# Moving a block inverse, small copies and squares between GpSimd, VectorE and ScalarE, and a planner that tracks reuse, in a hybrid RWKV-7 and retention decoder layer

## The chip, the core and the metric

The kernel runs on one core of a Trainium2 chip. A core has TensorE (matrix products into PSUM banks), VectorE (DVE), ScalarE (ACT), GpSimd (POOL) and SyncE (SP, which issues all DMAs here); each works through its own instructions in the order in which they are written, and they wait for each other on semaphores. The metric is the device time of one execution in microseconds; the kernel before takes 1558.78 us (median of three runs, the fastest 1557.02).

## What is computed

One layer of a decoder for 304 token rows: 16 meta tokens, a prompt of 256 and 8 samples of 4 tokens.

```python
xn = rms_norm(x, norm_mix)
z = xn @ w_in                       # 2048 -> 3360 + 4096 columns
o_a, S_a = rwkv7_mixer(z_a, ...)    # 16 heads of 64, delta rule state
o_b, S_b = retention_mixer(z_b, ...)  # 4 heads of 256
h = x + concat([o_a, o_b]) @ w_out
hn = rms_norm(h, norm_ffn)
h = h + (silu(hn @ w_gate) * (hn @ w_up)) @ w_down   # 5632 wide
y = rms_norm(h, norm_final)
```

The RWKV part is, per head and token, `S = S * w + (S a) b^T + v k^T` and `out = S r`. The kernel does it in blocks ("units") of 64 tokens (the first of 16), which needs the inverse of a unit lower triangular 64 x 64 matrix for each unit and head.

## The kernel before, in words

All activations are held transposed: features on the 128 partitions, the 304 (later 288) tokens in the free dimension. `main` (L634) walks over all weights in one fixed sequence (`steps`, L123): input projections in the order of `ORDER` (L54: the RWKV head pairs p0 to p7, the retention heads r0 to r3 and their gates g0 to g3 mixed), then the output projection, then the feed-forward part. A weight tile of 128 x 128 is used in three matmuls, because every fp32 value is split into a rounded half and a rest: hi x xh, hi x xl, lo x xh. ScalarE makes the half (`cast`, L617: the tile `wh`, four batches of 512 columns ahead, five buffers) and VectorE the rest (`rest`, L629: the tile `wl`). Weights come by SP into three buffers of 1024 columns (`wr`). Results collect in two PSUM banks, `acc`; the six other banks, `mm`, are for everything else. Nearly all other tiles lie in one arena, which the profile calls `arena_dt.float` (`arena_dt.float32r` for the rounded halves), so it can't tell them apart by name. All instructions are recorded by one helper, so they have one line, L302.

Beside `main` run streams, written as Python generators; each `yield` is a place where another stream, or `main`, may be written next. A pair of RWKV heads is the stream `pair` (L906): decays, normalised keys, clearing and filling the operand tiles (the fills are ScalarE copies, L988 to 993, and GpSimd copies, L995 to 1004), score matrices, then `inverse` (L1095), `units` (L1172, five units one after the other, a chain of small matmuls and copies), `sample` (L1219, the 8 decode sequences) and `pair_out` (L1297, group norm and gate). `mixed` (L803) shifts and mixes the projected rows of the RWKV part, and copies the last rows to `shout`, an output. `ret` (L1379) is a retention head. These streams all run beside the input projections, in the first 600 us; the output projection begins shortly before that.

`inverse` works on 5 units of a pair at a time, both heads on the partitions, 128 x [5, 64]. It cuts the diagonal 16 x 16 blocks out (`rb`, L1101, one `tensor_reduce`, L1106), forms their inverse by 15 steps of substitution, and combines blocks to 32 and to 64 by matmuls (L1150 to 1169). In the substitution, VectorE spreads row s of the blocks over the partitions by `stream_shuffle` (15 of 80 columns, in three groups of five), and GpSimd does, for each s, a multiply and an add on 5 x (15 - s) columns, which each need the one before.

`rsqrt` (L705) gives 1/sqrt by an integer estimate and two steps of Newton's kind, all on VectorE, nine instructions. It is called once for the first norm (304 columns), in each pair for the keys (312 columns, with `floor`) and for the group norm (288), in each retention head (288), and twice on three columns (`rstd_from`, L1556).

The order is set by `Plan` (L307). The kernel is built twice. In the draft, `book` (L348) gives every instruction a start and an end, from a cost for each engine, from when the engine is free, and from when what its operands hold is ready; `pick` (L426) writes the next step of the first stream that is due by TensorE's clock, and otherwise a step of `main`. The second time the same choices are replayed and the arena's places are those that `Room` found from the draft's times. Two things in it matter here. `follows` (L334) is meant to make a new use of a PSUM bank or a buffer wait for the last use of what lay there, and `banks` to know which tiles lie in PSUM. Both are keyed by tile names: `t` (L573) hands in the name that it asks for (`mm_0`), while `book` looks up the name that the tile carries, to which the allocator has appended a running number (`mm_0_58`). So neither is ever found, and the planner takes reused banks and buffers as free at once.

Of the kernel before, what the change touches and what calls it, by code (L numbers as in the profile page):

```python
# [12 lines left out]
ALU = mybir.AluOpType  # L13
# [293 lines left out]
class Plan:  # L307
# [5 lines left out]
    def __init__(self, nc, rooms, draft, log, keep):  # L313
# [5 lines left out]
        self.mode, self.parts, self.empty, self.begun, self.idle = None, {}, 0.0, 0.0, 0.0  # L319
        self.streams, self.made = [], 0  # L320
# [27 lines left out]
    def book(self, eng, what, a, k):  # L348
# [20 lines left out]
        else:  # L369
            part = out.shape[0] < P  # L370
            each = sum(math.prod(x.shape[1:]) == 1 for x in ins) if n > 1 else 0
            if eng == "DVE":
                big = max(math.prod(x.shape[1:]) for x in aps)
                per = 0.56 if what == "tensor_scalar" and ins[0].name not in self.banks else 1.05
                dur, tail = {"stream_shuffle": (148, 90), "transpose": (95 + 1.02 * n, 80), "tensor_reduce": (40 + 1.8 * big, 85),
                             "tensor_tensor_scan": (65 + 2.1 * n, 85)}.get(what, (62 + per * n + 67 * each, 83))
            elif eng == "ACT":
                dur, tail = 108 + 0.83 * n + 90 * each - 40 * (ins[0].name in self.banks), 94
            else:
                dur, tail = (60 + 0.85 * n, 60) if what == "memset" else (185 + 0.8 * n, 60) if what == "tensor_copy" else (265 + 2 * n, 60)  # L380
# [14 lines left out]
        self.end = max(self.end, done + 100)  # L395

# [142 lines left out]
class Step:  # L539
# [33 lines left out]
    def t(self, shape, tag, dt=F32, bufs=None, pool=None):  # L573
        self.n += 1
        if pool is not None:
            name = f"{tag}_{self.n}"
            if tag in ("mm", "acc"):
                self.plan.banks.add(name)
            old = self.tags.setdefault(tag, [])
            old.append(name)  # L580
            n = {"mm": 8 - ACC, "acc": ACC}.get(tag, bufs)
            if n and len(old) > n:
                self.plan.follows(name, old[-1 - n])
            return pool.tile(shape, dt, tag=tag, name=name, **({} if bufs is None else {"bufs": bufs}))
# [120 lines left out]
    def rsqrt(self, src, scale, eps, floor=None, out=None):  # L705


        dve = self.dve
# [24 lines left out]
    def start(self):  # L733
# [3 lines left out]
        self.dve.memset(self.ones, 1.0)  # L737
        xh, xl = self.xh, self.xl
# [1031 lines left out]
```

## Time and profile before

| | us |
|---|---|
| median of the runs | 1558.78 |
| the profiled execution's own time | 1558.99 |
| its span, first to last instruction | 1557.1 |
| TensorE busy, in the span | 1535.6 |
| VectorE busy | 1102.0 |
| ScalarE busy | 821.4 |
| GpSimd busy | 179.2 |

The profile's page names engines as PE (TensorE's matmuls), PEld (its weight loads, which overlap them), DVE, ACT, POOL and SP. A row of a group reads: line, engine, operation, written tile <- read tiles, shape and count, then busy us, mean ns of one, and idle us of that engine just before, with who ended it. Matmuls are pipelined and their ends are modelled, so a busy PE can still stand for parts of a microsecond. A row of the waits reads: who waited <- for whom: us in total, times, longest. fp32 matmuls of the `mm` kind are recorded as two passes.

### The profile page before, as it was taken

What the parts mean: (1) busy time and instruction counts of PE and PEld (TensorE: products, weight loads), DVE (VectorE), ACT (ScalarE), POOL (GpSimd) and SP (SyncE); (2) the same over time, 40 slices, a digit from 0 to 9 for tenths busy, and PEclk for the clock granted to TensorE, in tenths of its full rate; (3) what the DMA queues carried; (4) which work ended last, traced back from release to release, by engine and by line L of the source; (5) the groups of instructions that cost most, each with busy time, mean ns of one, the idle gap of its engine ahead of it and who ended that gap; (6) DMA issues with size and microseconds to landing.
All of it is one profiled execution on the core that took longest, in us unless ns stands there. A gap on an engine that the chain in (4) does not pass through costs nothing.

```text
span 1557.1 us, 30803 instructions
## 1 busy us (share of the span) xinstructions
PE 1535.6 (99%) x11388; PEld 1505.7 (97%) x11388; DVE 1102.0 (71%) x2590; ACT 821.4 (53%) x1795; POOL 179.2 (12%) x567
## 2 busy tenths in 40 slices
PE   9999999999999999999999999999999999999997
PEld 8999999998999999999999999999999999999997
DVE  7999888996999786676555565555565656565657
ACT  6766776766676555455444444444444444444445
POOL 0454415513143000000000000000000000000000
PEclk9999999999999999999999999999999999999999
DMA  7443443434545546755555555555555555555553
GB/s 249 154 136 119 127 130 120 115 107 152 181 143 176 170 143 238 243 167 161 164 173 163 174 156 172 162 165 169 168 163 172 164 166 164 171 166 166 161 176 118
DMA packets 76997, 252.48 MB, mean 162 GB/s; under 512 B 9392, under 2 KB 14640, under 8 KB 76848
## 3 DMA queue, kind: packets, MB, share of 16 engines
q1 hardware_dynamic: 76848, 250.52, 51.5%
q8 instruction: 90, 1.47, 0.4%
q14 instruction: 59, 0.48, 0.1%
HBM read 236.21 MB, written 14.28 MB: 161 GB/s over the span
## 4 chain that ended last, share of the span: by engine, by line
PE 85%; DVE 11%; issue 1%; ACT 1%; DMA 1%; POOL 0%; SPq 0%; DVEq 0%; ACTq 0%; POOLq 0%
PE acc L302 76%; PE mm L302 9%; DVE arena_dt.float L302 8%; DVE wl L302 3%; ACT arena_dt.float L302 1%; DMA arena_dt.float<-xT 0%; POOL arena_dt.float L302 0%; DMA arena_dt.float<-lora 0%; ACT wh L302 0%; DVE arena_dt.float32r L302 0%; DMA wr<-big 0%; ACT arena_dt.float32r L302 0%; SPq L302 0%; DVEq L1766 0%; ACT xh L302 0%
## 5 line engine op out<-in xcount | busy, mean ns | idle before, releaser
L302 PE MATMUL acc<-xh,wh 128*128 128x288 f32 (+2 forms) x2592 | 790.9, 305 | 0.0
L302 PE MATMUL acc<-xh,wl 128*128 128x288 f32 (+2 forms) x2592 | 769.9, 297 | 0.9 <-DVE wl L302 0.8
L302 PE MATMUL acc<-xl,wh 128*128 128x288 f32 (+2 forms) x2592 | 766.7, 296 | 0.0
L302 ACT CAST wh<-wr 128x512 fp32r<-128x512 f32 x826 | 501.6, 618 | 373.2 <-PE acc L302 343.3
L302 DVE TENSOR_TENSOR wl<-wr,wh 128x512 fp32r<-128x512 f32 x826 | 563.3, 690 | 114.5 <-ACT wh L302 112.1
L302 PEld LDWEIGHTS acc<-xh,wh 128*128 128x128 f32 x2592 | 487.7, 188 | 4.8 <-issue 1.5
L302 PEld LDWEIGHTS acc<-xl,wh 128*128 128x128 f32 x2592 | 486.9, 188 | 4.0 <-issue 0.7
L302 PEld LDWEIGHTS acc<-xh,wl 128*128 128x128 f32 x2592 | 486.0, 188 | 2.0 <-DVE wl L302 1.5
L302 PE MATMUL acc<-arena_dt.float32r,wh 128*128 128x288 f32 x1408 | 280.0, 294 | 0.4 <-ACT arena_dt.float32r L302 0.3
L302 PEld LDWEIGHTS acc<-arena_dt.float32r,wh 128*128 128x128 f32 x1408 | 225.5, 188 | 0.9 <-ACT arena_dt.float32r L302 0.6
L302 PE MATMUL acc<-arena_dt.float32r,wl 128*128 128x288 f32 x704 | 207.0, 294 | 0.0
L302 DVE TENSOR_TENSOR arena_dt.float<-acc,arena_dt.float 128x288 f32<-128x288 f32 (+4 forms) x181 | 72.7, 420 | 167.6 <-PE acc L302 167.3
L302 PE MATMUL mm<-arena_dt.float 128*128 128x128 f32 (+7 forms) x1072 | 168.4, 317 | 6.2 <-DVE arena_dt.float L302 4.9
L302 DVE TENSOR_TENSOR arena_dt.float<-arena_dt.float 128x288 f32<-128x288 f32 (+11 forms) x483 | 159.5, 354 | 11.7 <-ACT arena_dt.float L302 6.2
L302 DVE TENSOR_TENSOR arena_dt.float<-arena_dt.float,acc 128x288 f32<-128x288 f32 x208 | 94.4, 454 | 100.8 <-PE acc L302 100.6
L302 PEld LDWEIGHTS mm<-arena_dt.float 128*128 128x128 f32 (+1 forms) x1072 | 138.2, 182 | 20.6 <-issue 9.3
L302 ACT ACTIVATE arena_dt.float<-arena_dt.float 128x288 f32<-128x288 f32 (+6 forms) x200 | 85.0, 432 | 119.5 <-DVE arena_dt.float L302 118.2
L302 PEld LDWEIGHTS acc<-arena_dt.float32r,wl 128*128 128x128 f32 x704 | 132.7, 189 | 0.0
L302 ACT COPY arena_dt.float<-mm 64x64 f32<-64x64 f32 (+8 forms) x330 | 91.1, 287 | 72.6 <-PE mm L302 62.4
L302 POOL TENSOR_TENSOR arena_dt.float<-arena_dt.float 128x75 f32<-128x75 f32 (+14 forms) x240 | 94.5, 394 | 100.4 <-DVE arena_dt.float L302 75.6
L302 ACT CAST arena_dt.float32r<-arena_dt.float 128x288 fp32r<-128x288 f32 (+4 forms) x73 | 30.5, 424 | 102.2 <-DVE arena_dt.float L302 89.6
L302 POOL COPY arena_dt.float<-arena_dt.float 128x32 f32<-128x32 f32 (+5 forms) x123 | 35.6, 321 | 125.9 <-DVE arena_dt.float L302 74.0
(64 smaller groups left out, 676.0 us busy)
## 6 DMA issues: line engine op xcount, KB each, us to landing
wr<-big SPq DMA_DIRECT2D x409, 512.0 KB, 3.5
arena_dt.float<-s0r SPq DMA_DIRECT2D x16, 512.0 KB, 6.4
out_rts<-arena_dt.float SPq DMA_DIRECT2D x16, 512.0 KB, 5.4
arena_dt.float<-xT SPq DMA_DIRECT2D x4, 576.0 KB, 6.5
out_y<-arena_dt.float SPq DMA_DIRECT2D x8, 288.0 KB, 2.2
arena_dt.float<-xT SPq DMA_DIRECT2D x7, 304.0 KB, 5.6
wr<-big SPq DMA_DIRECT2D x8, 256.0 KB, 5.3
arena_dt.float<-lora SPq DMA_DIRECT2D x16, 128.0 KB, 3.7
```

The lines of the kernel that those rows point to most:

```text
L302: return self._plan.keep(f(*a, **k))
```

## The change

Five things are changed together.

1. `inverse`: the 15 steps' multiplies and adds go from GpSimd to VectorE, with a `yield` after each step; the shuffles write only the columns that are used later; the reduction becomes two adds; the initial copy goes to ScalarE.
2. `rsqrt`: for more than 64 columns the squares, and the first scaling where there is no floor, go to ScalarE. The arithmetic is written as y * (c*d - c*x*y*y), twice; narrow calls keep nine VectorE instructions.
3. Small copies in `mixed`, `pair` and `sample` go from GpSimd to ScalarE; two copies to `shout` become one. GpSimd keeps clears only.
4. `t` hands the planner the name that the tile carries, so that reuse of banks and buffers, and which tiles lie in PSUM, are known to the draft.
5. The planner's costs are changed, and `share` is new: it keeps VectorE instructions that read two SBUF tensors and GpSimd's from overlapping in the draft.

```diff
             if eng == "DVE":
...
-                dur, tail = {"stream_shuffle": (148, 90), "transpose": (95 + 1.02 * n, 80), "tensor_reduce": (40 + 1.8 * big, 85),
+                dur, tail = {"stream_shuffle": (62 + 1.05 * n, 90), "transpose": (95 + 1.02 * n, 80), "tensor_reduce": (40 + 1.8 * big, 85),
...
-            if part and eng != "POOL":
+            if part and eng == "DVE":
                 dur += 80
+            if part and eng == "ACT" and (each or n == 320):
+                dur += 10 if ins[0].name not in self.banks else -90
             self.started = max(self.clock[eng], at)
-            self.clock[eng] = at = self.started + dur
+            at = self.share(eng, what, ins, self.started, dur, each) + dur
+            self.clock[eng] = at
...
+    def share(self, eng, what, ins, at, dur, each):
+        there = [x for x in ins if x.name not in self.banks and math.prod(x.shape[1:]) > 1]
+        if eng == "DVE" and (len(there) > 1 or there and what == "tensor_scalar"):
+            for s, e in self.taken["POOL"]:
+                if s <= at < e:
+                    at = e
...
-            name = f"{tag}_{self.n}"
+            ap = pool.tile(shape, dt, tag=tag, name=f"{tag}_{self.n}", **({} if bufs is None else {"bufs": bufs}))
             if tag in ("mm", "acc"):
-                self.plan.banks.add(name)
+                self.plan.banks.add(ap.name)
             old = self.tags.setdefault(tag, [])
-            old.append(name)
+            old.append(ap.name)
             n = {"mm": 8 - ACC, "acc": ACC}.get(tag, bufs)
             if n and len(old) > n:
-                self.plan.follows(name, old[-1 - n])
+                self.plan.follows(ap.name, old[-1 - n])
...
+        wide = n > 64
         if floor is not None:
             dve.tensor_scalar(x, src, floor, None, op0=ALU.max)
+        elif wide:
+            act.activation(x, src, AF.Identity, scale=scale, bias=self.eps[eps][:m])
+            yield
...
-        dve.tensor_mul(a, x, y)
-        yield
-        dve.scalar_tensor_tensor(a, a, -0.703952253, y, op0=ALU.mult, op1=ALU.mult)
-        dve.scalar_tensor_tensor(y, a, 0.703952253 * 2.38924456, y, op0=ALU.add, op1=ALU.mult)
-        yield
-        dve.scalar_tensor_tensor(a, x, -0.5, y, op0=ALU.mult, op1=ALU.mult)
-        dve.tensor_mul(a, a, y)
-        yield
-        dve.scalar_tensor_tensor(y, a, 1.5, y, op0=ALU.add, op1=ALU.mult)
+        for c, d in (0.703952253, 2.38924456), (0.5, 3.0):
+            if wide:
+                yield
+                act.activation(a, y, AF.Square)
+                yield
+                dve.scalar_tensor_tensor(a, a, -c, x, op0=ALU.mult, op1=ALU.mult)
+            else:
+                dve.tensor_mul(a, x, y)
+                yield
+                dve.scalar_tensor_tensor(a, a, -c, y, op0=ALU.mult, op1=ALU.mult)
+            dve.scalar_tensor_tensor(y, a, c * d, y, op0=ALU.add, op1=ALU.mult)
...
-        self.pool.tensor_copy(zb[:, :, 0], self.shin[:m, i, :])
+        self.act.copy(zb[:, :, 0], self.shin[:m, i, :])
...
-        self.pool.tensor_copy(self.shout[:m, i, 0:1], z[:m, NP:NP + 1])
-        self.pool.tensor_copy(self.shout[:m, i, 1:], zb[:, :, 4])
+        self.act.copy(self.shout[:m, i, :], z[:m, NP::5])
...
-        pool.tensor_copy(ax[:, :, 0:4], smp(ra[:, 0, :]))
+        act.copy(ax[:, :, 0:4], smp(ra[:, 0, :]))
...
-        dve.tensor_reduce(rr, rb.rearrange("p u q c -> p u c q"), axis=AX.X, op=ALU.add)
+        dve.tensor_add(rb[:, :, :2], rb[:, :, :2], rb[:, :, 2:])
+        yield
+        dve.tensor_add(rr, rb[:, :, 0], rb[:, :, 1])
...
-                dve.stream_shuffle(rs[:, s - c[0]], rr, [16 * (i // 16) + s for i in range(32)])
+                dve.stream_shuffle(rs[:, s - c[0], :, s + 1:], rr[:, :, s + 1:],
+                                   [16 * (i // 16) + s for i in range(32)])
             yield
             for s in range(*c):
-                pool.tensor_mul(tm[:, :, s + 1:], rs[:, s - c[0], :, s + 1:],
-                                x[:, :, s:s + 1].to_broadcast([P, NU, 15 - s]))
-                pool.tensor_add(x[:, :, s + 1:], x[:, :, s + 1:], tm[:, :, s + 1:])
+                dve.tensor_mul(tm[:, :, s + 1:], rs[:, s - c[0], :, s + 1:],
+                               x[:, :, s:s + 1].to_broadcast([P, NU, 15 - s]))
+                dve.tensor_add(x[:, :, s + 1:], x[:, :, s + 1:], tm[:, :, s + 1:])
+                yield
```

The other copies in `pair` (L997 to 1004, L1050), `inverse` (L1103) and `sample` (L1271, L1272) are changed in the same way, from `pool.tensor_copy` to `act.copy`.

More of the change, by code (lines that the diff above doesn't have):

```diff
@@ L319, in __init__ @@
         self.mode, self.parts, self.empty, self.begun, self.idle = None, {}, 0.0, 0.0, 0.0
+        self.taken = {"DVE": [], "POOL": []}
         self.streams, self.made = [], 0
@@ L395, in book @@
         self.end = max(self.end, done + 100)
+    def share(self, eng, what, ins, at, dur, each):
[4 more added lines that the diff above has]
+                    at = e
+            held = self.taken["DVE"]
+            if held and not each and at - held[-1][1] < 60:
+                held[-1] = held[-1][0], at + dur - 52
+            else:
+                held.append((at, at + dur - 52))
+        elif eng == "POOL" and what != "memset":
+            for s, e in self.taken["DVE"]:
+                if s - 28 <= at < e:
+                    at = e
+            self.taken["POOL"].append((at + 28, at + (80 if what == "tensor_copy" else dur)))
+        else:
+            return at
+        del self.taken[eng][:-20]
+        return at
     def array(self, what, out, w, x, ready):
@@ L737, in start @@
         self.dve.memset(self.ones, 1.0)
+        self.eps = {}
+        for e in {RMS_EPS, GN_EPS, 4 * RMS_EPS}:
+            self.eps[e] = self.t([P, 1], f"eps{len(self.eps)}", pool=self.cp)
+            self.pool.memset(self.eps[e], e)
         xh, xl = self.xh, self.xl
@@ L993, in pair @@
             act.copy(arp[h, 1:, :, hi], units(ra[h]))
[L995 to L998 removed]
+        act.copy(ax[:, :, 0:4], smp(ra[:, 0, :]))
+        act.copy(ax[:, :, 5:9], smp(ra[:, 1, :]))
+        act.copy(bs[:, 0], smp(bk[:, 0, :]))
+        act.copy(bs[:, 1], smp(bk[:, 1, :]))
         dl = self.t([P, NU], "dl")
[L1000 to L1002 removed]
+        act.copy(dl[:, 0:1], dd[:, META - 1:META])
+        act.copy(dl[:, 1:], dd[:, UB[1] + 63:NP:64])
+        act.copy(d4, smp(dd)[:, :, 3:4])
         for hi, h in enumerate(HALF):
[L1004 removed]
+            act.copy(axd[h, :, hi, :], ax[h])
         yield
@@ L1049, in pair @@
             yield
-        pool.tensor_copy(four(o[:, SEQ:]), self.xs_of.pop(p)[:, :, 5:9])
+        act.copy(four(o[:, SEQ:]), self.xs_of.pop(p)[:, :, 5:9])
         yield
@@ L1102, in inverse @@
         x = self.t([P, NU, 16], "xe")
-        pool.tensor_copy(x, cst("i16", 16)[:, None, :].to_broadcast([P, NU, 16]))
+        act.copy(x, cst("i16", 16)[:, None, :].to_broadcast([P, NU, 16]))
         yield
         rr = self.t([P, NU, 16], "rr")
-        dve.tensor_reduce(rr, rb.rearrange("p u q c -> p u c q"), axis=AX.X, op=ALU.add)
+        dve.tensor_add(rb[:, :, :2], rb[:, :, :2], rb[:, :, 2:])
+        yield
+        dve.tensor_add(rr, rb[:, :, 0], rb[:, :, 1])
         yield
@@ L1270, in sample @@
         sb = self.t([P, 2, 2, 32], "sb")
-        pool.tensor_copy(four(sb[:, 0, 0, :]), xs[:, :, 0:4])
-        pool.tensor_copy(four(sb[:, 0, 1, :]), smp(v))
+        act.copy(four(sb[:, 0, 0, :]), xs[:, :, 0:4])
+        act.copy(four(sb[:, 0, 1, :]), smp(v))
         for q in range(2):
```

14 lines of the change are left out of this document (4 added, 10 removed).

## The prediction

> **What bounds the kernel now.** I read the page's busy line first, then stages.
>
> ```profile
> span 1557.1 us, 30803 instructions
> PE 1535.6 (99%) x11388; PEld 1505.7 (97%) x11388; DVE 1102.0 (71%) x2590; ACT 821.4 (53%) x1795; POOL 179.2 (12%) x567
> PE 85%; DVE 11%; issue 1%; ACT 1%; DMA 1%; POOL 0%; SPq 0%; DVEq 0%; ACTq 0%; POOLq 0%
> ```
>
> TensorE is never long without work. The third line is the chain that ended last: 11% of it, some 170 us, runs over VectorE. The windows view splits the span there (columns: span, then busy us and count of PE, PEld, DVE, ACT, POOL, granted clock, DMA share, GB/s).
>
> ```profile
> 0.00:15.00 15.00, 12.53 (x57) 11.67 (x58) 8.35 (x17) 10.20 (x20) 0.54 (x6) 0.89 0.86 303
> 15.00:600.00 585.00, 576.74 (x4186) 549.25 (x4184) 509.83 (x1500) 389.51 (x1016) 178.70 (x561) 1.00 0.47 151
> 600.00:1540.00 940.00, 939.58 (x7096) 938.47 (x7095) 574.53 (x1052) 419.18 (x755) 0.00 (x0) 1.00 0.55 167
> 100.00:150.00 50.00, 49.08 (x361) 46.99 (x361) 45.64 (x152) 36.09 (x101) 20.61 (x63) 1.00 0.39 123
> 300.00:350.00 50.00, 49.66 (x358) 47.61 (x358) 47.17 (x147) 33.32 (x94) 15.51 (x52) 1.00 0.39 114
> 450.00:500.00 50.00, 48.98 (x362) 45.49 (x361) 48.13 (x140) 34.97 (x97) 16.74 (x52) 1.00 0.41 130
> ```
>
> GpSimd works only before 600 us, so all that the change moves lies there. From 600 us on, the weight load (PEld) is busy 938.5 of 940 us: nothing can be won there, and no changed line does much there. From 15 to 600 us it is idle for 585 - 549.25 = 35.75 us. That is the ceiling of any gain, since the change neither adds nor removes a matmul. VectorE is at 510 of 585 us (87%), up to 48.1 of 50 in one window; ScalarE at 67%.
>
> The waits view for 15 to 600 us says what TensorE stood for (total us, times, longest); of the weight load's rows, those under "issue" (12.8 us) name no releaser:
>
> ```profile
> PE mm L302 <- DVE arena_dt.float L302: 4.9, 5, 2.4
> PE mm L302 <- ACT arena_dt.float L302: 1.6, 2, 0.9
> PE acc L302 <- DVE wl L302: 0.8, 1, 0.8
> PE mm L302 <- POOL arena_dt.float L302: 0.3, 1, 0.3
> PEld mm L302 <- issue: 10.5, 27, 2.6
> PEld acc L302 <- issue: 2.3, 8, 0.4
> PEld mm L302 <- PE acc L302: 3.7, 8, 1.2
> PEld acc L302 <- DVE wl L302: 1.5, 3, 1.0
> PEld mm L302 <- ACT arena_dt.float L302: 1.5, 3, 0.9
> PEld mm L302 <- PE mm L302: 1.4, 5, 0.4
> PEld mm L302 <- POOL arena_dt.float L302: 1.0, 2, 0.8
> ```
>
> Named waits: 4.9 + 1.6 + 0.8 + 0.3 = 7.6 us of matmuls, and 3.7 + 1.5 + 1.5 + 1.4 + 1.0 = 9.1 us of weight loads, together 16.7 us if none is counted twice. The longest has a sequel:
>
> ```profile
> 367.67 1.13 PE L302 MATMUL mm<-arena_dt.float 128*128 128x128 f32 x8 [2.41 <-DVE arena_dt.float L302]
> 368.00:372.50 4.50, 4.50 (x42) 2.27 (x41) 2.33 (x6) 2.32 (x7) 0.00 (x0) 0.62 0.96 301
> ```
>
> After 2.41 us without a matmul the granted clock is 0.62 for 4.5 us: 4.5 x 0.38 = 1.7 us more.
>
> **The change, part by part.** GpSimd gives up its arithmetic and copies and keeps the clears:
>
> ```profile
> L302 POOL TENSOR_TENSOR arena_dt.float<-arena_dt.float 128x75 f32<-128x75 f32 (+14 forms) x240 | 94.5, 394 | 100.4 <-DVE arena_dt.float L302 75.6 <-issue 6.8
> L302 POOL COPY arena_dt.float<-arena_dt.float 128x32 f32<-128x32 f32 (+5 forms) x123 | 35.6, 321 | 125.9 <-DVE arena_dt.float L302 74.0 <-PE mm L302 27.8 <-DMA arena_dt.float<-shift 21.2
> L302 POOL COPY shout<-arena_dt.float 128x1 f32<-128x1 f32 (+3 forms) x54 | 22.4, 449 | 132.6 <-DVE arena_dt.float L302 132.6
> L302 POOL COPY arena_dt.float<-cst 128x80 f32<-128x80 f32 x8 | 2.2, 277 | 0.2
> 290.62 0.53 DVE L302 TENSOR_TENSOR arena_dt.float<-arena_dt.float 128x64 f32<-128x64 f32 x4
> L302 DVE TENSOR_TENSOR arena_dt.float<-arena_dt.float 128x64 f32<-128x64 f32 x48 | 11.3, 236 | 0.2
> L302 DVE TENSOR_TENSOR arena_dt.float<-arena_dt.float 128x16 f32<-128x16 f32 x48 | 8.7, 182 | 0.7
> L302 DVE STREAM_SHUFFLE arena_dt.float<-arena_dt.float 128x80 f32<-128x80 f32 x120 | 20.8, 241 | 0.0
> L302 DVE TENSOR_REDUCE arena_dt.float<-arena_dt.float 128x80 f32<-128x320 f32 x8 | 5.7, 714 | 0.0
> L302 DVE TENSOR_TENSOR arena_dt.float<-arena_dt.float,cst 128x160 f32<-128x160 f32 x8 | 2.5, 317 | 0.0
> ```
>
> *Pieces of the inverse.* 240 multiplies and adds of 5 to 75 columns (40 on average) go to VectorE. Four independent small ones took 0.53 us, so at least 240 x 0.13 = 32 us; one alone takes 0.18 to 0.24 us, so at most 240 x 0.21 = 50 us. Each here needs the one before, so I take the end nearer to the whole duration, 45 us. Behind a piece that waits for its predecessor stands all other VectorE work, wl subtractions and evacuations above all, and for those TensorE waits. But the generator now hands over after each pair of pieces, so they can be written in between, and wl is written some three batches of 12 matmuls ahead of its use; without that cover the chain of 30 x 0.21 = 6.3 us would stop TensorE once per pair. *Reduction:* 0.714 us becomes two adds, of 160 and 80 columns, about 0.317 + 0.25: -1.1 us in 8 pairs. *Shuffles:* half the columns, 0 to -6 us of the 20.8; I take -3.
>
> *Inverse square roots.* 21 wide ones: 8 of 312 columns give two multiplies to ScalarE, 12 of 288 and one of 304 give those and the first scaling.
>
> ```profile
> L302 DVE TENSOR_TENSOR arena_dt.float<-arena_dt.float 128x312 f32<-128x312 f32 x72 | 33.0, 478 | 0.5
> L302 DVE TENSOR_TENSOR arena_dt.float<-arena_dt.float 128x288 f32<-128x288 f32 x52 | 23.6, 464 | 0.9 <-ACT arena_dt.float L302 0.2
> L302 DVE TENSOR_SCALAR arena_dt.float<-mm 128x288 f32<-128x288 f32 x11 | 5.0, 453 | 2.0 <-PE mm L302 2.0
> L302 ACT ACTIVATE arena_dt.float<-arena_dt.float 128x288 f32<-128x288 f32 x16 | 7.1, 444 | 13.3 <-DVE arena_dt.float L302 13.2
> L302 ACT COPY arena_dt.float<-arena_dt.float 64x16 f32<-64x16 f32 x16 | 3.2, 200 | 0.1
> L302 ACT COPY arena_dt.float<-arena_dt.float 128x32 f32<-128x32 f32 x8 | 1.7, 218 | 5.4 <-DVE arena_dt.float L302 4.4 <-POOL arena_dt.float L302 0.9
> L302 DVE TENSOR_SCALAR arena_dt.float<-arena_dt.float 128x312 int32<-128x312 int32 x16 | 6.7, 419 | 0.3
> L302 DVE TENSOR_SCALAR arena_dt.float<-arena_dt.float 128x304 int32<-128x304 int32 x2 | 0.6, 320 | 0.1
> ```
>
> VectorE loses 16 x 0.478 + 13 x (0.453 + 2 x 0.464) = 25.6 us; ScalarE gains 16 + 39 = 55 instructions, 55 x 0.45 = 25 us. Each wide root now crosses from VectorE to ScalarE and back two or three times; what is late next is only that pair's or head's own stream, and TensorE has projections to do meanwhile. *Copies.* 123 + 54 + 8 = 185 on GpSimd become 158 on ScalarE (the two to shout are joined): 158 x 0.21 = 33 us. Three small clears for the scaling's constants go to GpSimd long before their use: nothing. ScalarE goes to 389.5 + 58 = 447 of 585 us, 76%. Behind a copy that waits stand the wh casts, made four batches ahead; that lead hides it, and without it each late copy would cost TensorE its own wait.
>
> *GpSimd out of VectorE's way.* The same integer instruction takes 0.419 us at 312 columns, where GpSimd often works, and 0.320 at 304: -0.1 us in each. Over some 50 instructions that is 5 us; ends 0 and 8.
>
> VectorE's sum: 45 - 1.1 - 3 - 25.6 - 5 = +10 us; ends 32 - 1.1 - 6 - 25.6 - 8 = -9 and 50 - 1.1 - 25.6 = +23.
>
> The Trainium skill ("VectorE: DVE Perf Modes", errata section) speaks against small pieces: each instruction pays a fixed 58 cycles besides one per column, at 0.96 GHz. An estimate from that page: 240 x 98 / 0.96 GHz = 25 us for the pieces, below my lower end; by it the time below would be 1547.
>
> *The plan.* Bank and buffer reuse now reach the planner, which before took a reused bank for free and an ACT cast for unhindered. A matmul is written when its inputs and its bank are due. Of the 16.7 us of waits I let half go, 0 to 16.7 being the ends: -8.4 us; of the 1.7 us at low clock half as well: -0.9.
>
> *On the path.* VectorE's +10 us counts where the chain runs over it: 170 of 585 us, 0.29: +2.9 (ends -2.6 and +23). ScalarE has 1% of the chain: 58 x 0.01 = +0.6.
>
> Sum: -8.4 - 0.9 + 2.9 + 0.6 = -5.8 us. The profiled execution took 1558.99 us (span 1557.1), the median is 1558.78, practically equal: **1553 us**.
>
> **Rivals.**
> *All waits go.* VectorE is freed more than I count, and TensorE waits for nothing named: -16.7 - 1.7, so 1540.6. For it: GpSimd copies of one column take 0.449 us in the mean and are plainly held up by someone; against it: VectorE's wl rows hardly stretch, and part of the waits is the data's own order. By the Trainium skill ("SBUF — State Buffer", section "Who interferes with whom") a GpSimd instruction that reads and a VectorE one with two inputs exclude each other for their whole length; by that rule this case comes about, and the ceiling stays where it is. The trace shows the lock mostly from GpSimd's side.
> *One order for another.* The new order has as many waits in other places, and the planner's view was near enough: 1557 to 1561, say 1559. For it: 16.7 us in 585 is already little.
> *VectorE becomes the bound (slower).* In windows where VectorE is above 0.9 (of those shown: 100, 300 and 450 us), the inverse's chain sits in its queue ahead of accumulator evacuations; with two accumulators TensorE stops when both are full. It decides once a window passes 48 of 50 us. Price: the upper end, +23 us, in half of the stage: +12, nothing won: 1571. Against it: at 48.13 of 50 TensorE still did 48.98.
>
> **How the numbers follow.** Forecast 0.42 (own range 1546 to 1557), all waits go 0.20, one order for another 0.20, VectorE the bound 0.15, others 0.03. The range runs from a little below the first rival, 1535, to near the third, 1569. A measurement tells about 2%, 31 us: faster by that needs 31 of the 35.75 us of idle weight load (0.04); slower by that is more than VectorE's upper end (0.05); within it 0.91.
>
> **What would show it.** Right: PEld's idle between 15 and 600 us falls from 36 to about 30 us, named waits to about 8; VectorE's busy time there is 510 to 530 us, ScalarE's near 447; GpSimd shows only MEMSET; the 240 pieces have means of 0.18 to 0.25 us; the stage from 600 to 1540 us is unchanged. Wrong: VectorE above 533 us with waits on wl or on accumulators (the third rival), matmul waits as long as before (the second), or any gain behind 600 us.

## The result and the profile after

The changed kernel takes 1567.69 us (median of four runs, 1567.21 to 1568.03), the kernel before 1557.02, 1557.30 and 1558.78 us beside it: a ratio of 1.0064, 95% interval [1.0044, 1.0084]. (One more run of before, at 2514.36 us, was disturbed and is left out; it was among the three whose median, 1558.78 us, the forecast started from, which is therefore about 1 us too high.) The forecast of 1553.0 named the wrong sign: 5.8 us were to be won, and some 10 were lost (0.0064 of 1558). The profiled execution took 1568.03 us. The head of its page:

```profile
span 1566.0 us, 30584 instructions
PE 1545.0 (99%) x11388; PEld 1509.6 (96%) x11388; DVE 1097.1 (70%) x2783; ACT 861.7 (55%) x2008; POOL 27.9 (2%) x145
PE 72%; DVE 3%; ACT 3%; issue 1%; DVEq 0%; ACTq 0%
```

VectorE lost 4.9 us of work and GpSimd 151, and TensorE is busy for 9.4 us more with the same 11388 matmuls. The chain that ended last holds 3% of VectorE where it held 11%, so by that view VectorE has let go, and still the time rose. The windows of the first 15 us and of the two stages:

```profile
0.00:15.00 15.00, 13.04 (x68) 11.56 (x69) 8.35 (x17) 10.06 (x20) 5.41 (x34) 1.00 0.86 299
15.00:600.00 585.00, 577.40 (x4133) 546.49 (x4132) 504.52 (x1691) 427.40 (x1224) 22.47 (x111) 1.00 0.46 148
600.00:1540.00 940.00, 939.61 (x7075) 936.98 (x7075) 567.56 (x1040) 414.99 (x748) 0.00 (x0) 1.00 0.55 169
```

Read the counts. In the first stage, which I call the mixing, 4133 matmuls were done where before did 4186, and the weight load stands idle for 585 - 546.49 = 38.5 us, not 30. In the second stage, where nothing was to change, TensorE is as busy as before (939.6 of 940 us) and yet did 7075 matmuls in place of 7096: each takes longer. So there are two losses. To measure them apart I number the matmuls on the projections' weights (`wh` or `wl`) in order of start. No. 3300, at the end of the output projection, starts at 663.1 us before and at 667.7 after (+4.6); the last, no. 9935, at 1542.5 and 1550.8 (+8.3). So the feed-forward part lost 3.6 us (883.1 against 879.5 from the one to the other). For the mixing 4.6 is too little, because the two executions differ before it begins: over its first 15 us the one of before ran at a granted clock of 0.89 (the first row of the windows in the prediction), the one of after at 1.00, and no. 100 starts at 23.6 us there and at 22.3 here. Counted from no. 100 to no. 3300, the mixing takes 639.5 us before and 645.4 after: 5.9 us lost, which with the 3.6 makes 9.5 of the 10. Below I compare the mixing in this way. The waits of the first stage:

```profile
PE mm L302 <- ACT arena_dt.float L302: 3.0, 7, 0.7
PE mm L302 <- DVE arena_dt.float L302: 1.5, 3, 0.7
PE mm L302 <- ACT wh L302: 1.4, 1, 1.4
PEld mm L302 <- ACT arena_dt.float L302: 12.0, 33, 0.9
PEld mm L302 <- issue: 4.2, 10, 0.9
PEld mm L302 <- PE acc L302: 2.3, 7, 0.8
PEld mm L302 <- ACT wh L302: 1.6, 1, 1.6
PEld mm L302 <- DVE arena_dt.float L302: 0.7, 3, 0.2
```

VectorE's long matmul waits (4.9 us, longest 2.4) have shrunk to 1.5, and no wait here is as long as the one that the lower clock followed. In their place stand 33 short waits of the weight load on ScalarE, 12.0 us instead of 1.5. (Part of this is a change of name: the weight load's waits under "issue", without a releaser, fell from 12.8 us to 6.5.) The costs of single edits:

```profile
L302 DVE STREAM_SHUFFLE arena_dt.float<-arena_dt.float 128x75 f32<-128x75 f32 (+14 forms) x120 | 16.0, 208 | 0.1
L302 DVE TENSOR_TENSOR arena_dt.float<-arena_dt.float 128x75 f32<-128x75 f32 x16 | 3.7, 234 | 0.3
L302 DVE TENSOR_TENSOR arena_dt.float<-arena_dt.float 128x5 f32<-128x5 f32 x16 | 2.7, 167 | 0.3
L302 DVE TENSOR_SCALAR arena_dt.float<-arena_dt.float 128x312 int32<-128x312 int32 x16 | 5.1, 320 | 0.5
L302 ACT COPY arena_dt.float<-mm 64x64 f32<-64x64 f32 x112 | 23.1, 206 | 15.3 <-PE mm L302 13.8
```

The pieces are the fifteen forms from 128x75 down to 128x5, 234 to 167 ns each; the integer instruction at 312 columns takes 0.320 us where it took 0.419 beside a working GpSimd. The last row becomes important below.

### The profile page after: what moved, and what is told of

Its sections match the earlier page's. It is cut to its first block, busy times and chain, and to the rows that moved or that the text cites. A ratio compares the mean times of both kernels' runs of the same rounds, so it can differ in the third digit from the quotient of the medians.

```text
span 1566.0 us, 30584 instructions
## 1 busy us (share of the span) xinstructions
PE 1545.0 (99%) x11388; PEld 1509.6 (96%) x11388; DVE 1097.1 (70%) x2783; ACT 861.7 (55%) x2008; POOL 27.9 (2%) x145
## 4 chain that ended last, share of the span: by engine, by line
PE 72%; DVE 3%; ACT 3%; issue 1%; DVEq 0%; ACTq 0%
PE acc L302 67%; PE mm L302 6%; DVE arena_dt.float L302 2%; ACT arena_dt.float L302 2%; DVE wl L302 1%; ACT wh L302 0%; ACT arena_dt.float32r L302 0%; DVE arena_dt.float32r L302 0%; DVEq L1807 0%; ACT shout L302 0%; ACTq L302 0%; DVEq L302 0%
## 5 line engine op out<-in xcount | busy, mean ns | idle before, releaser
L302 DVE TENSOR_TENSOR arena_dt.float<-arena_dt.float 128x288 f32<-128x288 f32 (+23 forms) x697 | 179.7, 288 | 12.0 <-ACT arena_dt.float L302 5.2
L302 PE MATMUL mm<-arena_dt.float 128*128 128x128 f32 (+5 forms) x1072 | 170.3, 312 | 4.0 <-ACT arena_dt.float L302 2.6
L302 ACT ACTIVATE arena_dt.float<-arena_dt.float 128x288 f32<-128x288 f32 (+6 forms) x242 | 103.9, 436 | 118.9 <-DVE arena_dt.float L302 117.2
L302 ACT COPY arena_dt.float<-mm 64x64 f32<-64x64 f32 (+11 forms) x330 | 91.9, 287 | 68.7 <-PE mm L302 62.1
L302 ACT COPY arena_dt.float<-arena_dt.float 128x32 f32<-128x32 f32 (+9 forms) x219 | 55.5, 301 | 10.8 <-DVE arena_dt.float L302 9.7
L302 DVE SCALAR_TENSOR_TENSOR arena_dt.float<-arena_dt.float 128x288 f32<-128x288 f32 (+3 forms) x100 | 43.8, 441 | 3.3 <-ACT arena_dt.float L302 1.5
```

The source lines that it names most:

```text
L302: return self._plan.keep(f(*a, **k))
```

## Experiments: where the feed-forward part loses 3.6 us

Nothing that the change does lies in that stage, but it adds three constants ("eps", 32 bytes each in a partition) ahead of the weights' buffers, which move `wr`, `wh`, `wl` and the arena by 96 bytes. The window from 750 to 1500 us holds only feed-forward matmuls, so its counts are paces. Before, then after:

```profile
750.00:1500.00 750.00, 750.00 (x5674) 750.00 (x5674) 441.94 (x790) 315.88 (x552) 0.00 (x0) 1.00 0.55 166
```
```profile
750.00:1500.00 750.00, 750.00 (x5650) 750.00 (x5649) 438.40 (x785) 313.99 (x547) 0.00 (x0) 1.00 0.54 166
```

750/5674 is 132.2 ns from start to start, 750/5650 is 132.7, both at a granted clock of 1.00.

**The constants alone**, put into the kernel before, and **the constants in one aligned tile**, in the kernel after.

```diff
 # b1: the kernel before, with
+        self.eps = {}
+        for e in {RMS_EPS, GN_EPS, 4 * RMS_EPS}:
+            self.eps[e] = self.t([P, 1], f"eps{len(self.eps)}", pool=self.cp)
+            self.pool.memset(self.eps[e], e)
 # a1: the kernel after, with one tile for the three
+        one = self.t([P, 16], "eps", pool=self.cp)
...
-            self.eps[e] = self.t([P, 1], f"eps{len(self.eps)}", pool=self.cp)
+            self.eps[e] = one[:, len(self.eps):len(self.eps) + 1]
```

> The kernel before with the three unused constants of the change added (three tiles, three clears by GpSimd), nothing else: the weight tiles start 32 bytes off a multiple of 64. Theory A: 5 to 6 us slower than before, about 1564 us, 753 matmuls per 100 us in the feed-forward stage. Theory B: 1558 us as before, 757 per 100 us.

> The changed kernel with its three scaling constants in one tile of 64 bytes a partition in place of three tiles of 32 bytes each: the weight tiles wh, wl, wr lie 32 bytes lower than in the changed kernel and start at multiples of 64 bytes again, as before the change; the instructions are the same. Theory A (the shifted addresses make every matmul 0.4% slower, 753 instead of 757 matmuls in 100 us of the feed-forward stage): 9900 weight matmuls x 0.55 ns = 5.5 us come back, about 1562 us, and the feed-forward stage shows 757 per 100 us again. Theory B (the slower rate belongs to the chip or the run, and the loss is one of order and waits): no difference to the changed kernel, 1567 us, 753 per 100 us.

Measured: b1 1562.72 us, ratio 1.0027 [1.0018, 1.0037]; a1 1569.99, ratio 1.0071 [1.0058, 1.0083]. The window of b1:

```profile
750.00:1500.00 750.00, 750.00 (x5651) 750.00 (x5650) 438.79 (x786) 314.34 (x549) 0.00 (x0) 1.00 0.54 166
```

This is after's count, with before's work: the shift alone costs the feed-forward stage 3.6 us, and the mixing nothing (639.5 us from no. 100 to 3300, as before). But the aligned tile doesn't repair it (5629 matmuls in the window, 133.2 ns each), so alignment to 64 bytes, as I had put it, isn't the rule, and a1 missed its theory A.

**A bench without the layer.** Chains of 48 matmuls on the same data, one place after another: d is where the weights lie, modulo 2048 bytes.

```python
for order in STEPS, STEPS[::-1]:      # d = 0, 32, ... 2016, up and down
    for d in order:
        gate(d)                       # 16 x (hi xh, hi xl, lo xh), 288 columns
for d in 768, 864:
    for e in STEPS:                   # e: where the moving operand lies
        down(d, e)
```

> The whole layer is left out: the kernel loads a few weights and runs only chains of 48 matmuls (128 x 128 weights on 288 columns, as in the feed-forward stage), the same data each time, with the weights' place d (bytes, modulo 2048) moved by 32 bytes from chain to chain, once up and once down, and then the moving operand's place e likewise. Theory 'place': the time from one matmul's start to the next depends on the places of the operands in SBUF. Then at d = 768 (the kernel before) the three kinds take 131.2, 131.7 and 133.8 ns in the mean (xh on wh, xl on wh, xh on wl), at d = 864 (the kernel after) 133.7, 131.4 and 132.4, up and down give the same numbers, and over all d the mean of the three moves by at least 1 ns. Rival 'load': the pace comes from what the other engines and the DMAs do at the time; then all d agree within 0.2 ns.

Worked out from the starts in the trace (last start minus first, over 47), in ns; all places that are equal modulo 256 agree within 0.05, but for the first one or two chains of a sweep, which are off by up to 1.1, and the table has the median of each:

```
d modulo 256            0      32     64     96     128    160    192    224
gate, going up        132.15 132.70 132.28 132.91 132.29 132.49 133.35 132.82
gate, going down      133.26 132.55 133.36 132.64 132.09 132.43 132.34 132.62
(e - d) modulo 256      0      32     64     96     128    160    192    224
down, for both d      132.81 133.36 133.11 133.13 132.28 132.09 132.43 133.30
```

No other engine works in those stretches, so the pace depends on the place: it repeats every 256 bytes, and for the down form only the distance between the operands counts. (In a sweep of gate chains the accumulator's bank changes along with the place, but places 128 bytes apart have the same bank: 64 and 192 going up still differ by 1.07 ns. Each down chain uses all four banks.) At d = 768 the three kinds take 131.0, 132.3 and 133.2 ns going up, at 864 134.2, 131.5 and 132.2 going down: within 0.6 of the numbers named. In the other direction they are up to 3 ns off, for one part of the expectation failed: up and down differ by 1.1 ns at 0 and 64. The accumulator's bank and what ran before differ between them. What ran before is enough to make such a difference: the first chain going up, at 0, follows chains at 0 and takes 133.26 ns, the others at 0 with the same bank follow a chain at 224 and take 132.15. Whether the bank matters too stays open. The Trainium skill ("SBUF — State Buffer", "Who interferes with whom") lets only the port pair of VectorE and GpSimd contend; that is said of engines that work at the same time, and these runs show 1% between places with both of them idle.

**The kernel after, with places chosen**: weights at 0 modulo 256 as before, the down projection's operand 160 behind them (64 in after).

```diff
 # c1: the kernel after, with
+        pad = self.t([P, 40], "pad", pool=self.cp)
+        self.pool.memset(pad, 0.0)
...
+                if dt == F32R:
+                    gap = self.mp.tile([P, 24], F32, tag="gap", name="gap")
+                    self.nc.gpsimd.memset(gap, 0.0)
```

> The kernel after, with 160 bytes more ahead of the weights' buffers and 96 bytes ahead of the arena of the FFN's activations, so that the weights lie at 0 modulo 256 (as in the kernel before; 96 in the kernel after) and the down projection's operand 160 bytes behind them modulo 256 (64 in the kernel after). Not one instruction of the work is changed. Theory 'place' (the bench: 132.17 ns from start to start at 0, 132.10 at 160): the feed-forward stage goes from 132.78 ns per matmul back to 132.2, which is 3.9 us over its 6635 matmuls, and the projections of the mixing gain up to 1.7 us: 1562 to 1564 us, weight-load waits on ScalarE unchanged near 12 us. Rival 'contention' (what VectorE and ScalarE do in the feed-forward stage slows TensorE): 1567 to 1570 us.

Measured: 1562.30 us, ratio 1.0030 [1.0019, 1.0041], against 1.0064 without.

```profile
750.00:1500.00 750.00, 750.00 (x5677) 750.00 (x5676) 440.60 (x788) 316.08 (x551) 0.00 (x0) 1.00 0.54 167
```

The pace is before's, no. 9935 starts 879.4 us after no. 3300, as in before (879.5), and the mixing gains 1.3 us too: 5.3 us by the ratios, with no instruction of the work changed. Weight-load waits on ScalarE stay at 12.1 us. So the loss of the feed-forward part comes from the places. c1 and the runs from c2 on, below, have both places at 0 and 160; all of them do 5677 or 5678 matmuls in that window, so that they differ in the mixing alone.

## Experiments: where the mixing loses

**First trials, parts undone.** I call the planner's costs its prices, `share` the lock, and the new inverse square roots the roots. These first runs have the places as they fell, so their times hold a loss in the feed-forward part too. b2 is before's work under the whole new planner; a2 is a1 with a planner that, as in before, never finds a name; a3 is after with before's inverse; a4 is after with its copies on GpSimd; a6 holds each stream back 300 ns.

```diff
 # a2: reuse and banks unknown, as in the kernel before
-            ap = pool.tile(shape, dt, tag=tag, name=f"{tag}_{self.n}", **({} if bufs is None else {"bufs": bufs}))
-            if tag in ("mm", "acc"):
-                self.plan.banks.add(ap.name)
...
-                self.plan.follows(ap.name, old[-1 - n])
-            return ap
+            return pool.tile(shape, dt, tag=tag, name=f"{tag}_{self.n}", **({} if bufs is None else {"bufs": bufs}))
 # a6
-            s[2] = self.end if self.end > s[2] else max(s[2], self.clock["PE"]) + 300
+            s[2] = self.end + 300 if self.end > s[2] else max(s[2], self.clock["PE"]) + 300
 # a3, a4: the lines of the change's diff for `inverse` (but its initial copy), and for the copies, taken back
```

> The kernel before with the changed planner alone (costs, shared port, names); all work stays on its old engine, addresses as before. Theory C: 3 to 8 us faster than before, 1551 to 1555. Theory D: 2 to 8 us slower, 1560 to 1566, with more waits of weight loads for ScalarE than the 1.5 us of before.

> As the run with aligned constants, and the planner again never finds the names of banks and buffers (what it did before the change); its new costs and the moved work stay. Theory C (knowing reuse helps, as the prediction said): slower than the aligned run by 3 to 8 us. Theory D (knowing reuse makes the planner place matmuls with less margin behind ScalarE's copies out of PSUM, which it now counts 40 ns cheaper, and so makes the 33 waits of weight loads for ScalarE): faster than the aligned run by 3 to 8 us, and waits of weight loads for ScalarE fall from 12 us to under 5.

> The kernel after with the inverse as before (one reduction, whole shuffles, multiplies and adds by GpSimd); all else as after. Places of the operands stay as in the kernel after, so the feed-forward stage keeps its pace up to the arena's own placement (1 to 2 us either way). Theory 'just in time' (the plan writes small matmuls right behind ScalarE's casts, and these short waits take what was won): the inverse is not what costs; 1564 to 1571 us, weight-load waits on ScalarE still 8 to 15 us, VectorE's busy time from 15 to 600 us lower by about 40 us. Rival 'pieces': the small pieces on VectorE delay casts and evacuations; then 1560 us or less and fewer waits.

> The kernel after with all its small copies back on GpSimd; all else as after. Theory 'just in time': the waits come from the plan's order, not from the copies; weight-load waits on ScalarE stay near 10 us, 1563 to 1569 us. Rival 'queue': the casts that feed the small matmuls stand behind the 158 new copies on ScalarE; then weight-load waits on ScalarE fall below 5 us and the mixing stage ends 4 us earlier, 1562 us or less.

> The kernel after, with the planner holding every stream back 300 ns longer before its next work is written. Theory 'just in time': the small matmuls are written where their inputs are 50 ns from ready, so 300 ns more cover the error of the planner's durations; weight-load waits on ScalarE fall from 12.0 to below 6 us and the mixing stage ends 3 to 5 us earlier: 1562 to 1565 us. Rival 'one order for another': as many waits come back elsewhere, or the mixing runs out of projections to fill in; 1566 to 1572 us.

| run | us | ratio to before | no. 100 to 3300 against before |
|---|---|---|---|
| b2 | 1567.02 | 1.0053 [1.0041, 1.0066] | +5.8 |
| a2 | 1619.55 | 1.0387 [1.0373, 1.0401] | +54.4 |
| a3 | 1570.31 | 1.0075 [1.0061, 1.0089] | +8.7 |
| a4 | 1566.85 | 1.0053 [1.0040, 1.0065] | +5.0 |
| a6 | 1595.51 | 1.0226 [1.0204, 1.0247] | +34.2 |

The planner alone makes before's work slower, by 5.8 us in the mixing (the rest of its 8 us is the feed-forward part, where another draft puts the arena's operands elsewhere); b2 speaks against my step "half go" by itself. The inverse in pieces isn't the loss: without it (a3) the mixing is 2.8 us longer than in after, and the time 1.7 us by the ratios, within their intervals. (VectorE's work in that stage fell by 21.8 us, not by the 40 that I expected of a3.) Nor are the copies: a4's mixing is 0.9 us shorter than after's, though a4's waits fall to little more than half:

```profile
PEld mm L302 <- ACT arena_dt.float L302: 6.8, 20, 0.7
```

a2 says that after's work needs a plan that knows the reuse; its loss, 49 us against a1, is far beyond the 3 to 8 that either theory named, and wasn't taken apart. a6 missed my expectation entirely; its window and two waits show how:

```profile
15.00:600.00 585.00, 556.64 (x3927) 524.36 (x3926) 484.49 (x1642) 414.22 (x1184) 28.81 (x137) 0.99 0.43 136
```
```profile
PEld mm L302 <- issue: 16.6, 28, 2.6
PEld mm L302 <- ACT arena_dt.float L302: 20.3, 27, 2.6
```

206 matmuls fewer fit in the stage than in after, spread over all of it, and the waits grow to 2.6 us. My reading, which no run tests, is that holding back every step of every stream stretches the streams themselves. Slack everywhere is no cure.

**Parts done alone.** c2 is the kernel before with the new roots only; c3 finds reused names, with before's prices; c4 has the new prices and the lock, with names unknown.

```diff
 # c2: rsqrt as in the change's diff, the three constants, pads of 160 and 32 bytes
 # c3: `t` as in the change's diff
 # c4: prices and `share` as in the change's diff
```

> The kernel before, with the inverse square roots of the kernel after alone (wide ones hand their squares to ScalarE); planner, inverse and copies as before, operands placed as in the run c1 (0 and 160). VectorE loses some 25 us in the mixing, ScalarE gains some 25. Theory 'TensorE is fed on time, its order decides': within 2 us of the kernel before, 1556 to 1560 us. Rival 'VectorE is the bound' (11% of the chain of waits lay on it): 25 x 0.29 = 7 us faster, 1551 us.

> The kernel before, with one half of the planner's change: it finds a reused bank or buffer by its real name. Durations as before, no lock between VectorE and GpSimd, places 0 and 160. Theory 'reuse makes the order tight' (streams are taken up only when their bank is due, and small matmuls then wait for ScalarE one after the other): mixing ends 4 us later as in the run with the whole new planner, 1562 to 1564 us. Rival 'the prices': 1557 to 1560 us.

> The kernel before, with the other half of the planner's change: new durations and the lock between VectorE and GpSimd; a reused bank or buffer still comes for free. Places 0 and 160. Theory 'reuse makes the order tight': near the kernel before, 1557 to 1560 us. Rival 'the prices' (shorter GpSimd and shuffle times let the plan write a small matmul too early): 1562 to 1564 us.

Measured: c2 1547.93 us, ratio 0.9935 [0.9923, 0.9948]; c3 1554.94, 0.9984 [0.9976, 0.9993]; c4 1559.32, 1.0013 [1.0004, 1.0022]. c3 came out below both of its ranges, against the theory that reuse makes the order tight; c4 fell into that theory's range, against the rival that blamed the prices. So neither theory held: each half of the planner's change alone is worth some 2 us, down and up, and only together (b2, +5.8 us in the mixing) do they cost more. The rival of c2 holds: the roots alone win 10 us, more than the 7 it named. c2 is also faster than both kernels. Its busy line, its window and two of its waits:

```profile
PE 1529.5 (99%) x11388; PEld 1501.9 (97%) x11388; DVE 1077.1 (70%) x2535; ACT 842.7 (55%) x1850; POOL 180.5 (12%) x572
```
```profile
15.00:600.00 585.00, 582.54 (x4253) 557.50 (x4252) 493.58 (x1463) 416.81 (x1084) 179.77 (x561) 1.00 0.46 152
```
```profile
PE mm L302 <- DVE arena_dt.float L302: 1.1, 3, 0.5
PEld mm L302 <- ACT arena_dt.float L302: 1.6, 4, 0.9
```

VectorE is lighter by 24.9 us, 67 matmuls more than in before fit in the stage, and the weight load's idle time falls from 35.75 to 27.5 us. Waits on VectorE drop without new ones on ScalarE. (The roots also hand over at other places, so the order changes with them; the run doesn't part the two.) So the loss isn't from the roots; the remaining parts must give some 14 us back (c1 stands at 1.0030).

**Back to the kernel after, part by part.** On top of c2: reuse by name (e1), then prices and lock (e2), then the inverse in pieces (e4); copies on top of that are c1. e3 puts the copies on e1.

```diff
 # e1 = c2 + `t` of the change        # e2 = e1 + prices and `share` of the change
 # e4 = e2 + `inverse` of the change (initial copy on GpSimd)
 # e3 = e1 + copies on ScalarE
```

> The kernel before with the new inverse square roots and with bank and buffer reuse found by name; durations, inverse and copies as before; places 0 and 160. Theory 'the gains add' (roots -9.7, reuse -2.6 us when tried alone): 1544 to 1547 us. Rival 'reuse makes the order tight once VectorE is free': 1549 to 1556 us, with over 15 short weight-load waits on ScalarE.

> The same with the new durations and the lock between VectorE and GpSimd too, so roots and the whole planner, without the inverse and the copies; places 0 and 160. Theory 'the new prices give the gain away' (with reuse they cost 7 us on the work of before): 1552 to 1557 us, weight-load waits on ScalarE near 10 us. Rival 'the inverse and the copies give it away': as the run before it, 1544 to 1548 us.

> The roots, reuse by name and the small copies on ScalarE; durations and inverse as before; places 0 and 160. Theory 'the new prices give the gain away': the copies cost 1 us, as in the kernel after: 1545 to 1549 us. Rival 'queue' (the copies stand ahead of casts on ScalarE): 1553 us or more.

> The kernel after with its small copies back on GpSimd, as in an earlier run, but at places 0 and 160. Theory 'place': 1561 to 1562 us, 5 us under that run. With the run of roots and planner it says what the inverse in pieces costs in the new plan: if 'the new prices give the gain away' holds, 5 to 9 us above that run's time are not left, but at most 4.

| kernel | us | ratio to before | step, from ratios x 1558 | no. 100 to 3300 |
|---|---|---|---|---|
| before | 1558 | 1 | | 639.5 |
| c2: + roots | 1547.93 | 0.9935 [0.9923, 0.9948] | -10.1 | 629.8 |
| e1: + reuse | 1550.61 | 0.9950 [0.9938, 0.9963] | +2.3 | 633.2 |
| e2: + prices and lock | 1565.82 | 1.0046 [1.0032, 1.0059] | **+15.0** | 647.8 |
| e4: + inverse in pieces | 1561.73 | 1.0023 [1.0014, 1.0031] | -3.6 | 643.6 |
| c1: + copies on ScalarE | 1562.30 | 1.0030 [1.0019, 1.0041] | +1.1 | 644.1 |
| after: places as they fell | 1567.69 | 1.0064 [1.0044, 1.0084] | +5.3 | 645.4 |

The steps add up to +10.0. They depend on the order in which they are added; and with intervals of some 0.0012 on each side, +2.3 and +1.1 don't stand out, and -3.6 does so barely. The step that decides is the planner's prices and lock. e1's time lies in its rival's range, but with 3 weight-load waits on ScalarE and not 15; e2's loss goes the way of its theory, but with 15 us against some 7 it is twice as large; e4 came out as named. (e4 beside a4, 1561.73 to 1566.85, is mostly the effect of the places once more.) e3, at 1559.78 us (1.0012 [1.0003, 1.0021]), missed its theory: under the old prices the same copies cost 9 us, and the rival named 1553 or more. Why they cost only 1 us under the new prices, where the waits are there already, isn't settled. Window and waits of e1, then of e2:

```profile
15.00:600.00 585.00, 581.62 (x4230) 555.11 (x4229) 490.77 (x1453) 415.07 (x1080) 175.42 (x561) 1.00 0.46 152
```
```profile
PEld mm L302 <- ACT arena_dt.float L302: 0.9, 3, 0.4
```
```profile
15.00:600.00 585.00, 573.57 (x4114) 542.78 (x4114) 485.12 (x1442) 407.79 (x1065) 174.45 (x561) 1.00 0.46 148
```
```profile
PEld mm L302 <- ACT arena_dt.float L302: 8.8, 24, 0.9
PE mm L302 <- ACT arena_dt.float L302: 3.5, 10, 0.6
```

The same work, written in another order: 3 weight-load waits on ScalarE become 24, and 116 matmuls fewer fit in.

**Which price.** The small matmuls of a unit read what ScalarE has just copied out of a bank. Of e2's 24 weight-load waits, 20 (7.2 of 8.8 us) end with a ScalarE instruction that reads a bank on 64 partitions, 10 of them with a 64 x 64 copy; of after's 33 it is 25 (9.6 of 12.0 us), of e1's 3 it is one. A 64 x 64 copy takes 206 ns by the row shown with the result. The planner of before allows 108 + 0.83 x 64 + 80 for it and 94 for landing, 335 ns; that of after, with the bank found (-40) and without the 80, allows 215. So the new price is right within 9 ns, and the old one was 129 too long; c4, where banks aren't found, allows 255. Behind that every planner adds 100 ns before TensorE uses the result; in e2's trace the 20 weight loads start 51 ns after the copy's end. Measured so, the new plan keeps 215 + 100 - 206 - 51 = 58 ns in hand at this place, and e1's 138. For one kind the new price is too short: 16 copies of 64 x 64 with a scale take 307 ns, and it allows 215 for them (five of the 20 waits):

```profile
L302 ACT ACTIVATE arena_dt.float<-mm,arena_dt.float 64x64 f32<-64x64 f32 x16 | 4.9, 307 | 1.1 <-PE mm L302 0.9
```

f1 is e2 with the 80 ns put back on every ScalarE instruction that writes part of the partitions (295 ns for the copy, as in e1; 385 for the copies with a scale, whose own term goes); f3 is e4 with the same.

```diff
-            if part and eng == "DVE":
+            if part and eng != "POOL":
                 dur += 80
-            if part and eng == "ACT" and (each or n == 320):
-                dur += 10 if ins[0].name not in self.banks else -90
```

> The run of roots and whole planner, with one price put back: copies of ScalarE on a part of the partitions are again planned 80 ns longer, as in the kernel before. A 64 x 64 copy from a bank takes 206 ns by the trace; the planner of before allowed 335 for it and its landing, the new one 215, this one 295. Theory 'margin' (the new prices are right, and so leave the small matmuls no slack behind the copy that feeds them; the old ones were wrong by some 100 ns, and that was the slack): the 15 us come back, 1549 to 1554 us, weight-load waits on ScalarE under 4 us. Rival 'lock or GpSimd's prices': 1562 to 1567 us, waits as in that run.

> The kernel after with its small copies on GpSimd, places 0 and 160, and the same price put back (with the copies on ScalarE as well the buffers no longer fit, so that is not built). Theory 'margin': 6 to 12 us under the same kernel without it (1561.7), so 1550 to 1556 us. Rival 'lock or GpSimd's prices': 1560 to 1564 us.

Measured: f1 1553.98 us, ratio 0.9978 [0.9969, 0.9987], where e2 had 1.0046; f3 1554.45, 0.9988 [0.9979, 0.9997], where e4 had 1.0023. By the ratios that is 10.6 us of the 15.0, and 5.5 us. Window and waits of f1:

```profile
15.00:600.00 585.00, 578.69 (x4214) 552.61 (x4212) 490.81 (x1451) 411.43 (x1074) 177.21 (x561) 1.00 0.46 152
```
```profile
PEld mm L302 <- ACT arena_dt.float L302: 4.4, 7, 1.3
PE mm L302 <- ACT arena_dt.float L302: 2.7, 4, 1.0
```

100 of the 116 matmuls are back, and the 24 waits are 7 (their 4.4 us are a little over the 4 that I named); those behind a bank read on 64 partitions are 5 instead of 20. f3's gain of 5.5 us is just under the 6 to 12 named. In the mixing, against before, the roots stand at -9.7 us where the plan allows 335 ns for the copy (c2), at -6.3 (e1) and -3.8 (f1) where it allows 295, and at +8.3 where it allows 215 (e2), though other things differ between these plans as well. So the surplus in an old, wrong price was slack in the place that needed it: between ScalarE's read of a bank and the matmul that uses it. The new prices took most of it away. Which of the repriced instructions matter most wasn't tried: the edit moves them all. The lock and the prices of GpSimd and the shuffles are left with some 4 us (f1 against e1), which weren't taken apart further.

## Why the prediction was wrong

*The ceiling* held: the best run, c2, won 10 us, well below the 35.75 us of idle weight load.

*Pieces of the inverse, 45 us.* The durations of the 240 sum to 47.6 us in e4's trace, yet VectorE's busy time rises by only 22.0 between e2 and e4:

```profile
PE 1539.5 (98%) x11388; PEld 1504.4 (96%) x11388; DVE 1079.0 (69%) x2535; ACT 842.5 (54%) x1850; POOL 175.2 (11%) x572
```
```profile
PE 1537.9 (99%) x11388; PEld 1503.5 (96%) x11388; DVE 1101.0 (71%) x2783; ACT 842.3 (54%) x1850; POOL 81.0 (5%) x332
```

With the reduction's -1.3 (5.7 us to two adds of 2.5 and 1.9) and the shuffles' -4.8 (20.8 to 16.0) taken out, the pieces add 22.0 + 6.1 = 28 us, 0.117 each, what GpSimd's silence saves elsewhere included. Their records overlap with those of other VectorE work: of the 1101.0 us in e4's trace, 1070.3 are left when the 240 are taken out, so they add 30.6. A row's mean is not what one adds. My "nearer to the whole duration" was the wrong end; my lower end, 32, was near. The estimate that the prediction took from the Trainium skill ("VectorE: DVE Perf Modes", errata section), 25 us, was too small, but the trace agrees with it better than with my 45.

*Inverse square roots:* -25.6 forecast, 1102.0 - 1077.1 = 24.9 measured. ScalarE's part is 21.3 (25 forecast); its 158 copies add 860.9 - 842.3 = 18.6 from e4 to c1 (33 forecast), though their durations in c1's trace sum to 33.9: the forecast was a sum of durations here too. So in the stage VectorE works 504.5 us and ScalarE 427.4 in after, both below what I named (510 to 530, near 447). c1's line:

```profile
PE 1538.6 (99%) x11388; PEld 1503.2 (96%) x11388; DVE 1097.1 (70%) x2783; ACT 860.9 (55%) x2008; POOL 28.0 (2%) x147
```

*On the path.* VectorE's sum was to be +10 and is -4.9. And the weight 0.29, its share of the chain (0.27, as 156 of its 170 us lie in the stage), was too low for the roots: 10.1 us for 24.9 is 0.4. A uniform share doesn't see what lies ahead of a wait; that the roots do is argued, not shown.

*The plan* is the step that failed: "Of the 16.7 us of waits I let half go, 0 to 16.7 being the ends". Its lower end was nothing, and I gave no reason that excluded a loss. With the low clock it was to give -9.3 us. On top of the roots the planner's parts gave +2.3 and +15.0. (The low clock is gone: after's windows from 0 to 1540 us show 1.00. But b1, with before's order, has the same wait, 2.34 us long, and a clock of 1.00 behind it; so the 1.7 us belong to the one execution of before, and no plan had to win them.) By the steps of the table the sum was +17.3 for the planner, -10.1 - 3.6 for VectorE's work, +1.1 for the copies and +5.3 for the places, where the forecast had -9.3, +2.9, +0.6 and nothing. I took a more accurate price for a better order. But a planner that writes work for the moment when it is due needs slack against what the draft doesn't see, and the wrong prices held it: 10.6 of the 15.0 us came back with those of ScalarE alone. The named waits went from 16.7 us to 22.5 by the rows shown, and from VectorE to ScalarE.

*Stage 600 to 1540 "unchanged", clears for "nothing".* The three constants cost no time to clear, but their 96 bytes cost 4.2 us where they alone are added (b1, 1.0027), and the places as they fell in the kernel after 5.3.

*Rivals.* "One order for another" is nearest to what the mixing did, but it saw no loss of this size (+4.6 us at equal places); its 1557 to 1561 us lie just below c1. "VectorE becomes the bound" was wrong in its sign: pieces on VectorE were a gain of 3.6 us. "All waits go" had its reason right, a freed VectorE, as c2 suggests, but the planner took it back. (Its 0.449 us is the mean of several forms: 0.458 for copies of one column to `shout`, 0.390 for those of eight.)

## What to carry to other kernels

Before making a planner's costs exact, find out what their errors were hiding: put a margin back at the one hand-over that TensorE waits for (80 ns on ScalarE's instructions on part of the partitions won 11 and 5.5 us here), not everywhere (300 ns on every stream lost 25 by the ratios). When a stage without a single changed line moves by a few tenths of a per cent, compare counts of matmuls in equal windows and then the operands' places in SBUF, before looking for contention. And test the parts of a joint change alone: of this one, the inverse square roots without the rest beat both kernels, 0.9935 [0.9923, 0.9948].

## What the runs showed of the hardware

The pace of back-to-back 128 x 128 by 288 column matmuls depends on where weights and moving operand lie, modulo 256 bytes: 132.09 to 133.38 ns in the bench with all other engines idle. Some places have two paces, 1.1 ns apart, and what ran before can choose between them. The kernel before, by the bench's down form at its distance of 224, should run at 133.30 there and runs at 132.22; b1 and a3, at the same distance, run at 133.30. What chose there wasn't found. A granted clock of 0.62 followed a wait of TensorE of 2.41 us in the kernel before, and none below 1.00 followed the same wait, 2.34 us, in b1. A 64 x 64 copy by ScalarE out of a bank takes 206 ns, and the weight load that waits for it starts 51 ns after its end.
